# Up-projection of a two-layer decoder: chunk 5 by seven products, and the input's sums begun on GpSimd before the first taps

## The chip, the cores and the metric

The kernel runs on one core of one Trainium2 chip. The metric is the time of one execution on the device in microseconds (us). The core has a matrix engine (TensorE, PE in the profile, with its weight loads shown apart as PEld), a vector engine (VectorE, DVE), a scalar engine (ScalarE, ACT), GpSimd (POOL) and a queue that only starts transfers (SyncE, SP). POOL can compute and can also start transfers. Each engine takes its instructions strictly from its own list; an instruction that has to wait holds up everything behind it on that list.

## The reference, cut to what matters

The model is a trunk of two layers over 512 tokens of width 1024, all in float32. Each layer has an attention part and a gated feed-forward part. The change is in the feed-forward part, which both layers have in the same shape:

```python
def conv_ffn(xn, w_up, cw, cb, w_down):
    a = xn @ w_up                       # (512, 1024) @ (1024, 5632)
    ap = jnp.pad(a, ((0, 0), (CONV_W - 1, 0), (0, 0)))
    a = sum(ap[:, j:j + T] * cw[j] for j in range(CONV_W)) + cb
    gate, val = jnp.split(a, 2, axis=-1)
    return (jax.nn.gelu(gate, approximate=True) * val) @ w_down
```

The 5632 columns of `w_up` are 2816 gate columns and 2816 value columns.

## The kernel before, in words

**Products in three parts.** A float32 product is made of three fast products: each operand is split into a rounded high part and the low remainder, and high x high, high x low and low x high are added up in PSUM (`mm3`, lines 263 to 266). A split costs a rounding copy on ACT (line 57) and a low part. The low part is either a subtraction on DVE (line 69) or, where the lists `ADDED` say so, a copy of the negated weights on ACT (line 64) to which a transfer from the POOL queue adds the raw weights (line 84, "accumulating transfer").

**Chunks.** The up-projection of a layer runs in 22 chunks, c = 0 to 21. A chunk is one block of 128 gate columns and one of 128 value columns. An ordinary chunk needs for each of its two blocks 8 steps of the depth times 3 products of 128x512: 48 matmuls. For chunks 0 and 1 `first_products` (line 533) works in halves of the tokens, since the input's last blocks are still being normalised and transposed.

**Chunks by seven products.** The chunks in `SEVEN` treat depth halves and token halves as a two-by-two scheme of Strassen's kind: seven half-size products instead of eight. Each is 4 steps times 3 matmuls of 128x256 (`half_mm`, line 909): 84 matmuls a chunk. They need sums of the weights and sums of the input.

- The weights' sums: `weights_a(c)` (line 679) makes the first two pairs (A11 and A12, S3 and S2), `weights_b(c)` (line 711) the other ones (S1 and S4, A22). Both are cut into steps by `yield`; in the loop of chunk c the steps of `weights_b(c + 1)` and `weights_a(c + 2)` are taken one at a time between other work (line 936). Two chunks of `SEVEN` that stand side by side are a pair. In the first of a pair, and in one that stands alone, three low parts come by accumulating transfers (`add_low`, lines 671 to 674); in the second of a pair DVE subtracts them (`sub_low`, line 677). Before, the list has four pairs (8 and 9, 11 and 12, 14 and 15, 17 and 18) and chunk 6 alone.
- The input's sums: `sums_in` (line 645), also cut by `yield`. Step one: two additions of 128x2048 on POOL (line 649), high plus low part of the input. Steps two and three: four additions and subtractions on DVE (lines 651, 652, 654, 655). Then four times a rounding copy on ACT and a subtraction on DVE (lines 660 and 661), which give `XA` and `XB`, each with a high part `xsh` and a low part `xsl`. The loop takes one step per block of an ordinary chunk, from chunk 2 on (line 1022). Step one thus stands in chunk 2, behind the first block's products in the text, the last one in chunk 5.

**What follows a chunk.** `taps` (line 610) makes the convolution from the two PSUM banks of the chunk before: per block one pass on ACT (line 614) and two on DVE (lines 615 and 617). `glu` applies the GELU on ACT (line 635), `product` multiplies gate and value on DVE (line 632), and the result goes to memory through the POOL queue (line 630).

**In a chunk by seven products** the order on PE is A11, S3, S2, A22, A12, S1, S4 (lines 952 to 990). DVE and ACT join partial results between these (lines 953, 955, 959, 979, 993, 999). A22 is added onto the bank that holds S3's result, so it may start only when line 955 has read that bank.

**What sets the order.** The text of the kernel is the order of each engine's list; there is no planner. Buffers come from pools with fixed numbers of slots (16 of 8 KB for split weights and inputs, 10 of 4 KB for raw weights, taps and weight sums); an instruction waits when its slot's last user isn't done. The raw weights come through the SP queue (line 49), each load waiting for a slot.

Of the kernel before, what the change touches and what calls it, by code (L numbers as in the profile page):

```python
# [24 lines left out]
BIG = 3.0e38  # L25


SEVEN = 6, 8, 9, 11, 12, 14, 15, 17, 18

ADDED = (4, 5, 7, 10, 13, 16, 20), (4, 5, 20, 21)  # L30
ND = NF // 2
LAST = 3

# [70 lines left out]
def trunk_kernel(ctx, tc, x, norm_gains, w_qkv_a, w_o_a, w_q_b, w_o_b, kv_norm, w_kvf, b_f,  # L104
# [11 lines left out]
    def t8(shape, dt=F32, name="t8"):  # L116
        return p8.tile(shape, dt, tag="t8", name=name)
# [487 lines left out]
    def ffn(l, bd, cp, nxt, ahead):  # L605
# [19 lines left out]
        def product():  # L625

            if gated:
                c, bb = gated.pop()
                if c - 1 in hc:
                    pool.dma_start(hD[c - 1], hc.pop(c - 1))  # L630
                hc[c] = t2([128, T], name="hc")
                dve.tensor_tensor(hc[c], bb[:, 0, :], bb[:, 1, :], ALU.mult)

        def glu(c, bb):
            act.activation(bb[:, 0, :], bb[:, 0, :], AF.Gelu_apprx_tanh)
            gated.append((c, bb))

        def post(c, banks, between=None):
            product()
            glu(c, taps(c, banks, between))  # L640
# [4 lines left out]
        def sums_in():  # L645

            v = [t8([128, 4, T], name=f"xsum{i}") for i in range(2)]
            for i in range(2):
                pool.tensor_tensor(v[i], xT[0][i].bitcast(F32), xT[1][i].bitcast(F32), ALU.add)
            yield  # L650
            dve.tensor_tensor(v[0][:, :, LO], v[0][:, :, HI], v[0][:, :, LO], ALU.subtract)
            dve.tensor_tensor(v[0][:, :, HI], v[1][:, :, HI], v[0][:, :, HI], ALU.subtract)
            yield
            dve.tensor_tensor(v[1][:, :, HI], v[1][:, :, HI], v[0][:, :, LO], ALU.subtract)
            dve.tensor_tensor(v[1][:, :, LO], v[1][:, :, LO], v[1][:, :, HI], ALU.subtract)
            yield
            for X, src in ((XA, v[0]), (XB, v[1])):
                X += [t8([128, 4, T], F32R, name="xsh"), t8([128, 4, T], F32R, name="xsl")]
                for k in (0, 2):
                    act.copy(X[0][:, k:k + 2], src[:, k:k + 2])  # L660
                    dve.tensor_tensor(X[1][:, k:k + 2], src[:, k:k + 2], X[0][:, k:k + 2].bitcast(F32), ALU.subtract)
                    yield
# [8 lines left out]
        def add_low(w, raw):  # L671

            act.activation(w[:, 1], raw, AF.Copy, scale=-1.0)
            pool.dma_start(w[:, 1], raw, accum_op=ALU.add)
# [4 lines left out]
        def weights_a(c):  # L679


            if c >= NF:
                return
            if c not in SEVEN:
                for i in range(2):
                    if c in ADDED[i]:
                        W.high_added()
# [9 lines left out]
            act.copy(w[0][:, 0], r0)  # L697
            if c - 1 not in SEVEN:
                add_low(w[0], r0)
# [3 lines left out]
            dve.tensor_tensor(sa[:, 512:1024], sb[:, 0:512], a11, ALU.subtract)  # L703
            if c - 1 not in SEVEN:
                act.copy(w[1][:, 0], sa)
# [5 lines left out]
        def weights_b(c):  # L711

            if c not in SEVEN:
                return
            (w0, w1), r0, a12, a22, sa, sb = rest.pop(c)
            if c - 1 in SEVEN:
                act.copy(w1[:, 0], sa)
# [3 lines left out]
            act.copy(w[1][:, 0, 0:512], a22)  # L721
            if c - 1 in SEVEN:
                sub_low(w1, sa)
# [195 lines left out]
        base = W.n_get  # L919
        first = first_products(bd, 4)  # L920
        xT = bd.xT
        post(0, first[0:2])
        post(1, first[2:4])
        W.ahead = 1
        W.split(base + 8)
        extra = sums_in()
        steps = iter(())
        begun = None
        before = None
        for c in range(2, NF):  # L930
            if c == NF - 4:
                pair_load(0)
            if c == NF - 3:
                sums = down_sums([(l, ND - 1), (1, 8 + l)], in_one, pool, 1, 0)
                next(sums)
            steps = chain(steps, weights_b(c + 1), weights_a(c + 2))
            if c in SEVEN:
                w = halves.pop(c)
                W.n_get += 2
                x11, x21, x22 = [(xT[0][i], xT[1][i], s) for i, s in ((0, LO), (1, LO), (1, HI))]  # L940
                if begun:
                    banks, s1, s17 = begun
                else:
                    banks = [bank([128, T], name="up") for _ in range(2)]
                    s1, s17 = (t2([128, 256], name="csum") for _ in range(2))
                s12 = t2([128, 256], name="csum")
                o1, o2, o3, o4 = banks[0][:, LO], banks[0][:, HI], banks[1][:, LO], banks[1][:, HI]

                def prod(o, a, x, start=False, w=w):
                    half_mm(o, w[a], x[0:2], x[2], start)  # L950

                def begin():
                    act.copy(s1, o1)
                    prod(o3, "S3", (*XA, HI), True)
                    dve.tensor_tensor(s17, o3, s1, ALU.add)
                    prod(o2, "S2", (*XB, HI))

                def join():
                    dve.tensor_tensor(s12, o2, s1, ALU.add)

                if begun:
                    prod(o2, "S2", (*XB, HI))
                    product()
                    join()
                    bb = taps(*before)
                else:
                    prod(o1, "A11", x11, True)
                    product()
                    bb = taps(*before, begin)
                    join()  # L970
                prod(o3, "A22", (*XB, LO))
                prod(o1, "A12", x21)
                prod(o2, "S1", (*XA, LO))
                next(steps, None)
                glu(before[0], bb)
                next(steps, None)
                if c + 1 in SEVEN:
                    next(steps, None)
                dve.tensor_tensor(o4, o2, s17, ALU.add)
                if c + 1 in SEVEN:  # L980
                    begun = ([bank([128, T], name="up") for _ in range(2)],
                             *(t2([128, 256], name="csum") for _ in range(2)))
                    b1, b3 = (o[:, LO] for o in begun[0])
                    prod(b1, "A11", x11, True, halves[c + 1])
                    act.copy(begun[1], b1)
                    prod(b3, "S3", (*XA, HI), True, halves[c + 1])
                else:
                    begun = W.get(), bank([128, T], name="up")
                    up(*begun, range(4))
                prod(o2, "S4", x22)  # L990
                if c + 1 not in SEVEN:
                    next(steps, None)
                dve.tensor_tensor(o3, o3, s12, ALU.add)
                if c + 1 in SEVEN:
                    late.pop()()
                    dve.tensor_tensor(begun[2], b3, begun[1], ALU.add)
                else:
                    next(steps, None)
                dve.tensor_tensor(o2, o2, s1, ALU.add)  # L999
            else:  # L1000
                banks = [bank([128, T], name="up") for _ in range(1 if begun else 2)]
                if begun:
                    w, first = begun
                    banks = [first, *banks]
                for s in range(2):
                    if s == 0 and begun:
                        up(*begun, range(4, KD))
                        begun = None
                    else:
                        up(W.get(), banks[s], range(KD))  # L1010
                    if c == NF - 2:
                        next(sums)
                    if s == 0 and before:
                        product()
                        bb = taps(*before, (lambda: pair_lows(0)) if c == NF - 1 else None)
                        next(steps, None)
                        glu(before[0], bb)
                        if c >= NF - 2:
                            pair_highs(c - NF + 2)
                            pair_sums(c - NF + 3)  # L1020
                    next(steps, None)
                    next(extra, None)

            if c + 1 not in SEVEN or c + 2 in SEVEN:
                run(steps)
            before = c, banks
            if c == NF - 3:
                pair_sums(0)
# [641 lines left out]
    for n in range(N + 3):  # L1670
        live = n < N
        if live:
# [3 lines left out]
            s = f_scores(j, i)  # L1676
# [83 lines left out]
```

## Time and profile before

| | us |
|---|---|
| median of three runs | 1116.84 |
| lowest and highest | 1116.65 and 1117.51 |
| the profiled execution | 1116.29 |
| its span, first to last instruction | 1114.5 |

The mean granted clock of TensorE in the profiled execution is 0.999. Besides the span, PE's busy time and the stretches of the up-projection matter here. Layer 0's feed-forward part begins with `first` at 179.80 us and its ordinary chunks 2 to 5 run from 204.55 us to 248.10 us; the one of layer 1 has chunk 2 start at 791.87 us.

A row of the timeline gives the start, the duration of all its merged instructions, the engine, the line, what is written and read, the shape and the count, and in brackets how long the engine was idle before it and who ended that. Matmuls overlap one another in the pipeline: a single one shows 0.39 us or 0.28 us, while the next starts 0.23 us or 0.12 us later. What a chunk costs is therefore read from start to start.

### The profile page before, as it was taken

What the parts mean: (1) busy time and instruction counts of PE and PEld (TensorE: products, weight loads), DVE (VectorE), ACT (ScalarE), POOL (GpSimd) and SP (SyncE); (2) the same over time, 40 slices, a digit from 0 to 9 for tenths busy, and PEclk for the clock granted to TensorE, in tenths of its full rate; (3) what the DMA queues carried; (4) which work ended last, traced back from release to release, by engine and by line L of the source; (5) the groups of instructions that cost most, each with busy time, mean ns of one, the idle gap of its engine ahead of it and who ended that gap; (6) DMA issues with size and microseconds to landing.
All of it is one profiled execution on the core that took longest, in us unless ns stands there. A gap on an engine that the chain in (4) does not pass through costs nothing.

```text
span 1114.5 us, 17752 instructions
## 1 busy us (share of the span) xinstructions
PE 1104.6 (99%) x6402; PEld 954.3 (86%) x6402; DVE 866.0 (78%) x1456; ACT 663.5 (60%) x1092; POOL 219.4 (20%) x321
## 2 busy tenths in 40 slices
PE   9999999999999999999999999999999999999997
PEld 6988889889999988888878888789989999988886
DVE  6567788577778799897697776848577778799894
ACT  5454575476666647576562688746465665647572
POOL 2832100421111121000001545500411111121000
PEclk9999999999999999999999999999999999999999
DMA  9469854388878899793447666374388878899862
GB/s 325 152 224 405 314 178 139 85 204 191 203 189 201 238 338 379 268 328 107 133 151 278 195 169 165 112 201 124 86 198 200 189 201 190 243 331 376 297 246 76
DMA packets 185521, 240.43 MB, mean 216 GB/s; under 512 B 11929, under 2 KB 131721, under 8 KB 185434
## 3 DMA queue, kind: packets, MB, share of 16 engines
q1 hardware_dynamic: 169594, 183.99, 50.5%
q0 software_dynamic: 15840, 55.32, 21.2%
q8 instruction: 50, 0.82, 0.3%
q14 instruction: 37, 0.30, 0.1%
HBM read 166.08 MB, written 39.63 MB: 185 GB/s over the span
## 4 chain that ended last, share of the span: by engine, by line
PE 94%; issue 2%; DVE 2%; POOL 1%; ACT 1%; DMA 0%; DVEq 0%; POOLq 0%
PE up L265 13%; PE up L264 13%; PE up L266 13%; PE acc L264 8%; PE acc L266 8%; PE acc L265 8%; PE qk_ps L265 2%; PE qk_ps L264 2%; PE qk_ps L266 2%; PE v_ps L264 2%; PE v_ps L266 2%; PE v_ps L265 2%; PE o_ps L1642 2%; PE s_ps L1594 1%; PE first L266 1%
## 5 line engine op out<-in xcount | busy, mean ns | idle before, releaser
L264 PE MATMUL acc<-w 128*128 128x512 f32 (+1 forms) x311 | 120.6, 388 | 0.3 <-DVE mix L326 0.3
L266 PE MATMUL acc<-w 128*128 128x512 f32 (+1 forms) x311 | 120.4, 387 | 0.0
L57 ACT CAST w<-wraw 128x1024 fp32r<-128x1024 f32 x102 | 104.8, 1048 | 15.7 <-PE v_ps L265 6.9
L69 DVE TENSOR_TENSOR w<-wraw,w 128x1024 fp32r<-128x1024 f32 x76 | 91.8, 1231 | 15.5 <-ACT w L57 15.0
L265 PE MATMUL acc<-w 128*128 128x512 f32 (+1 forms) x267 | 103.2, 387 | 0.0
L265 PE MATMUL up<-xbl,w 128*128 128x512 f32 (+1 forms) x284 | 99.2, 349 | 0.0
L265 PE MATMUL up<-xcl,w 128*128 128x512 f32 (+1 forms) x284 | 99.2, 349 | 0.0
L264 PE MATMUL up<-xbh,w 128*128 128x512 f32 (+1 forms) x284 | 99.1, 349 | 0.0
L264 PE MATMUL up<-xch,w 128*128 128x512 f32 (+1 forms) x284 | 99.1, 349 | 0.0
L266 PE MATMUL up<-xbh,w 128*128 128x512 f32 (+1 forms) x284 | 99.0, 349 | 0.0
L266 PE MATMUL up<-xch,w 128*128 128x512 f32 (+1 forms) x284 | 99.0, 349 | 0.0
L614 ACT ACTIVATE bb<-up,conv 128x512 f32<-128x512 f32 x80 | 59.8, 775 | 64.8 <-DVE up L999 33.6
L264 PE MATMUL up<-xsh,w 128*128 128x256 f32 x288 | 81.5, 283 | 0.0
L265 PE MATMUL up<-xsl,w 128*128 128x256 f32 x288 | 81.5, 283 | 0.0
L266 PE MATMUL up<-xsh,w 128*128 128x256 f32 x288 | 81.5, 283 | 0.0
L84 POOL DMA_DIRECT2D w<-wraw x26 | 24.7, 956 | 284.8 <-ACT w L64 248.4
L264 PEld LDWEIGHTS acc<-w 128*128 128x128 f32 x311 | 58.4, 188 | 12.5 <-DVE mix L326 0.7
L266 PEld LDWEIGHTS acc<-w 128*128 128x128 f32 x311 | 58.4, 188 | 11.9
L615 DVE SCALAR_TENSOR_TENSOR bb<-up,conv,bb 128x511 f32<-128x511 f32 x80 | 59.5, 744 | 7.1 <-ACT bb L614 7.1
L617 DVE SCALAR_TENSOR_TENSOR bb<-up,conv,bb 128x510 f32<-128x510 f32 x80 | 59.9, 749 | 2.8
L264 PEld LDWEIGHTS up<-xbh,w 128*128 128x128 f32 x284 | 53.8, 189 | 7.0
L264 PEld LDWEIGHTS up<-xch,w 128*128 128x128 f32 x284 | 53.8, 189 | 7.0
(315 smaller groups left out, 3165.5 us busy)
## 6 DMA issues: line engine op xcount, KB each, us to landing
wraw<-in_w_up_dram SPq DMA_DIRECT2D x88, 512.0 KB
w<-wraw POOLq DMA_DIRECT2D x36, 512.0 KB, 7.3
dT<-dsums SPq DMA_DIRECT2D x24, 512.0 KB
dsums<-in_w_down_dram SPq DMA_DIRECT2D x22, 512.0 KB
dsums<-in_w_down_dram SPq DMA_DIRECT2D x44, 256.0 KB
hD<-hc POOLq DMA_DIRECT2D x44, 256.0 KB, 7.2
dact<-hD SPq DMA_DIRECT2D x44, 256.0 KB
wraw<-dT SPq DMA_DIRECT2D x22, 512.0 KB
```

Of the source, the lines that this page charges most:

```text
L57: self.nc.scalar.copy(pair[:, 0], raw)
L69: self.nc.vector.tensor_tensor(pair[:, 1], raw, pair[:, 0].bitcast(F32), ALU.subtract)
L84: self.nc.gpsimd.dma_start(pair[:, 1], raw, accum_op=ALU.add)
L264: pe.matmul(o, ah, bh, start=first, stop=False, skip_group_check=shared)
L265: pe.matmul(o, ah, bl, start=False, stop=False, skip_group_check=shared)
L266: pe.matmul(o, al, bh, start=False, stop=last, skip_group_check=shared)
L614: act.activation(bb[:, s, :], ps, AF.Identity, bias=cp[:, 3, ch:ch + 1], scale=cp[:, 2, ch:ch + 1])
L615: dve.scalar_tensor_tensor(bb[:, s, 1:], ps[:, :T - 1], cp[:, 1, ch:ch + 1], bb[:, s, 1:], ALU.mult, ALU.add)
L617: dve.scalar_tensor_tensor(bb[:, s, 2:], ps[:, :T - 2], cp[:, 0, ch:ch + 1], bb[:, s, 2:], ALU.mult, ALU.add)
L1594: pe.matmul(s[hh][:, :nn], qT[j][:, m, hh, i * 128:(i + 1) * 128], k, start=m == 0, stop=m == 1)
L1642: pe.matmul(o[64 * hh:64 * hh + 64, i * 128:(i + 1) * 128], Vt[hd // 8][:, k, (hd % 8) * 64:(hd % 8) * 64 + 64], pT[j, i, hh][:, k, :], st ...
```

## The change

Chunk 5 joins `SEVEN`, so it is the first of a pair with chunk 6, which no longer stands alone; its two entries in `ADDED` go. There are then ten chunks by seven products per layer.

`sums_in` is started before the taps of chunk 0: its first step, the two additions on POOL, is now issued directly behind the first products and thus ahead of everything that POOL does for chunks 2 and later. The loop takes two steps instead of one behind each ordinary chunk's first block, so that steps two and three stand in chunk 2 behind its first block, the first `XA` step behind its second block, two more steps behind chunk 3's first block and the last one behind chunk 3's second block.

```diff
-SEVEN = 6, 8, 9, 11, 12, 14, 15, 17, 18
-
-ADDED = (4, 5, 7, 10, 13, 16, 20), (4, 5, 20, 21)
+SEVEN = 5, 6, 8, 9, 11, 12, 14, 15, 17, 18
+
+ADDED = (4, 7, 10, 13, 16, 20), (4, 20, 21)
@@ in ffn @@
         first = first_products(bd, 4)
         xT = bd.xT
+        extra = sums_in()
+        next(extra)
         post(0, first[0:2])
         post(1, first[2:4])
         W.ahead = 1
         W.split(base + 8)
-        extra = sums_in()
         steps = iter(())
@@ in the loop over chunks, behind an ordinary chunk's block s @@
                     next(steps, None)
                     next(extra, None)
+                    if s == 0:
+                        next(extra, None)
```

## The prediction, made before the changed kernel ran

> **What bounds the kernel now.** I read the page first (busy shares, slices, chain), then PE's own waits, then the stretches of the up-projection, then single rows.
>
> ```profile
> span 1114.5 us, 17752 instructions
> ...
> PE 1104.6 (99%) x6402; PEld 954.3 (86%) x6402; DVE 866.0 (78%) x1456; ACT 663.5 (60%) x1092; POOL 219.4 (20%) x321
> ...
> PEclk9999999999999999999999999999999999999999
> ...
> PE 94%; issue 2%; DVE 2%; POOL 1%; ACT 1%; DMA 0%; DVEq 0%; POOLq 0%
> ```
>
> ```profile
> PE warm L231 <- DVE zero L226: 1.4, 1, 1.4
> PE pT_ps L1627 <- ACT w L57: 0.6, 1, 0.6
> PE pT_ps L1627 <- DVE nm L1603: 0.4, 1, 0.4
> ```
>
> TensorE is busy 99% of the span at the full clock and carries 94% of the chain that ended last. Its longest waits are in the second fence, and none of these three is in an up-projection. So there is nothing to gain there by removing waits: time goes only if PE gets less to do, and it comes back at once if the change makes PE wait. The stretches say what a chunk costs:
>
> ```profile
> core 0: us, PE busy (x) PEld busy (x) DVE busy (x) ACT busy (x) POOL busy (x), PEclk, DMA share, GB/s
> 204.55:248.10 43.55, 43.55 (x194) 36.05 (x193) 29.99 (x32) 27.37 (x33) 17.13 (x12) 1.00 0.67 154
> 248.10:258.20 10.10, 10.10 (x80) 9.84 (x79) 7.79 (x13) 5.86 (x9) 2.28 (x3) 1.00 1.01 238
> 269.10:300.18 31.08, 31.08 (x217) 29.16 (x216) 25.03 (x40) 19.51 (x26) 5.12 (x9) 1.00 0.83 195
> ```
>
> ```profile
> 237.22 0.39 PE L264 MATMUL up<-xbh,w 128*128 128x512 f32 x1
> 248.10 0.28 PE L264 MATMUL up<-xbh,w 128*128 128x256 f32 x1
> 269.10 0.28 PE L264 MATMUL up<-xbh,w 128*128 128x256 f32 x1
> 300.18 0.28 PE L264 MATMUL up<-xbh,w 128*128 128x256 f32 x1
> 824.31 0.39 PE L266 MATMUL up<-xch,w 128*128 128x512 f32 x1
> 856.19 0.39 PE L266 MATMUL up<-xch,w 128*128 128x512 f32 x1
> 887.27 0.39 PE L266 MATMUL up<-xch,w 128*128 128x512 f32 x1
> ```
>
> The first stretch is the ordinary chunks 2 to 5: PE is busy all of its 43.55 us, 43.55 / 4 = 10.89 us a chunk, 10.89 / 48 = 0.227 us a matmul. The third is a pair and the ordinary chunk behind it (8, 9, 10), also without a gap: 31.08 us. The rows are the first matmuls of chunks 5, 6, 8 and 11, and in layer 1 the last matmuls ahead of chunks 5, 8 and 11.
>
> **The change part by part: PE.** Chunks 5, 6, 7 were ordinary, seven, ordinary, and become seven, seven, ordinary, which is what 8, 9, 10 are now. In layer 0 the three take 269.10 - 237.22 = 31.88 us before and should take 31.08 us: 0.80 us less. In layer 1 856.19 - 824.31 = 31.88 us against 887.27 - 856.19 = 31.08 us: 0.80 us again. By matmuls: 48 x 0.227 = 10.89 us go, and 84 x (31.08 - 10.89) / 168 = 10.10 us come. **Sum on PE: -1.6 us.** Everything else has to stay hidden under PE; whether it does is the rest of the work.
>
> **The additions on POOL** move past the POOL queue's transfers for chunk 4 and past the taps of chunks 0 and 1.
>
> ```profile
> L649 POOL TENSOR_TENSOR xsum<-xbh,xbl x2: 4934/4936/4937, 210.0 to 214.6; 128x2048 f32<-128x2048 f32 x2
> L651 DVE TENSOR_TENSOR xsum<-xsum x2: 5628/5628/5629, 215.0 to 802.1; 128x1024 f32<-128x1024 f32 x2
> L652 DVE TENSOR_TENSOR xsum<-xsum,xsum x2: 1225/1225/1225, 220.7 to 807.8; 128x1024 f32<-128x1024 f32 x2
> L660 ACT CAST xsh<-xsum x8: 1030/1035/1050, 226.5 to 832.9; 128x1024 fp32r<-128x1024 f32 x8
> L661 DVE TENSOR_TENSOR xsl<-xsum,xsh x8: 1218/1222/1226, 227.7 to 834.0; 128x1024 fp32r<-128x1024 f32 x8
> ```
>
> ```profile
> 28.23 1.11 POOL L1059 CAST xph<-xah 128x512 fp32r<-128x512 f32 x1
> 29.27 2.15 POOL L1059 CAST xpl<-xal 128x512 fp32r<-128x512 f32 x1
> 27.18 1.29 DVE L356 TENSOR_TENSOR xal<-xt_ps,xah 128x512 fp32r<-128x512 f32 x2 [1.28 <-ACT xah L355]
> 28.62 1.79 DVE L69 TENSOR_TENSOR w<-wearly,w 128x1024 fp32r<-128x1024 f32 x1 [0.16 <-ACT w L57]
> ```
>
> The two additions take 4.94 us each. Line 651 does the work of line 652 and takes 4.4 us longer, because it began beside the second addition. The other fence shows how such a meeting goes: DVE's subtraction (28.62 to 30.41) with both inputs in SBUF ran only once POOL's copy had ended at 29.34, and POOL's next copy, 2.15 us instead of 1.11 us, ran only once DVE was done. They take turns by whole instructions. The two subtractions of line 356, with one input in PSUM, lie beside POOL's copies at 0.64 us each: not held up.
>
> ```profile
> 190.55 1.29 DVE L356 TENSOR_TENSOR xbl<-xt_ps,xbh 128x512 fp32r<-128x512 f32 x2 [0.88 <-ACT xbh L355]
> 191.98 1.23 DVE L69 TENSOR_TENSOR w<-wraw,w 128x1024 fp32r<-128x1024 f32 x1
> 196.99 0.75 DVE L615 SCALAR_TENSOR_TENSOR bb<-first,conv,bb 128x511 f32<-128x511 f32 x1 [3.78 <-ACT bb L614]
> 201.75 0.69 DVE L632 TENSOR_TENSOR hc<-bb 128x512 f32<-128x512 f32 x1 [0.41 <-ACT bb L635]
> 207.02 1.22 DVE L69 TENSOR_TENSOR w<-wraw,w 128x1024 fp32r<-128x1024 f32 x1
> 219.11 1.23 POOL L84 DMA_DIRECT2D w<-wraw  x1
> ```
>
> The input's halves are complete at 191.2 us and 191.8 us (line 356). The first addition then runs from about 191.3 us to 196.2 us; line 69 behind line 356 waits for it and ends near 197.4 us instead of 193.2 us, where DVE was idle for 3.78 us; the taps start 0.4 us late. The second addition ends near 202.3 us, and line 632 waits about 0.5 us for it. Cost on the path: nothing, for the next chunks' weights that line 69 splits are used by PE at 215.4 us (204.55 + 10.89), and DVE is idle from 208.2 us. Were DVE kept out until both additions end, it would be 5 us late at 197 us and caught up near 212 us; still nothing. Nothing in the trace says when the two slots for the sums come free. If only with the end of the first products, at 204.55 us, the additions end near 214.4 us and the steps below are some 6 us later, which their cover of 12 us still holds. The accumulating transfer that stood behind the additions at 219.11 us goes out near 211 us.
>
> **The sums' DVE and ACT steps** run from 208.2 us, POOL no longer in their way. DVE has until chunk 5 starts at 237.2 us: four sums of 1.22 us, four of line 661 (4.9 us), two sets of taps (8 x 0.75 us), three products (0.69 us), and weight sums:
>
> ```profile
> L700 DVE TENSOR_TENSOR wsum<-wraw x5: 682/683/687, 232.3 to 297.6; 128x512 f32<-128x512 f32 x5
> L725 ACT CAST w<-wsum x4: 1052/1055/1058, 243.8 to 297.1; 128x1024 fp32r<-128x1024 f32 x4
> DMA to landing us min/median/max: 4.6/5.6/8.1
> ```
>
> Eight operations as line 700 (four sums and a half split for chunk 5, three sums for chunk 6): 5.4 us. Together 4.9 + 4.9 + 6.0 + 2.1 + 5.4 = 23.3 us in 29 us. In order: the four sums end near 213, the first XA subtraction at 214, the taps of chunk 2 near 218 (their second bank ends at 226.3 - 10.89 = 215.4), the first weight sums at 220, the last XB subtraction near 226. S3 and S2 need XA and XB at 238.7 us and 240.1 us: 12 us to spare. Cost: nothing.
>
> **The weights of chunk 5.** Gone per layer are two rounding copies, two negations and two transfers for chunk 5; three and a half copies, three negations, three transfers, five sums and the five small joins come. Chunk 6, now second of a pair, loses three negations and three transfers and gets three subtractions of 1.22 us on DVE. ACT's load hardly moves, POOL starts two transfers fewer, DVE gains about 8 us in work and loses the 4.4 us of line 651. The raw loads on SP are the same, at most one step later, and a chunk ahead of use. The latest piece is S1's low part. DVE's sum for it follows the taps of chunk 3, near 230 us; copy and negation (line 725, 1.05 us each) end near 232.3 us, and the transfer lands after 5.6 us, at most 8.1 us: 238 to 240.4 us. PE comes to S1 after five products, 237.2 + 5 x 10.10 / 7 = 244.4 us: 4 to 6.5 us to spare. Price if that cover goes: one for one, each microsecond beyond 244.4, in both layers. If it were merely as late as chunk 6's transfer stands now relative to its chunk, PE would still not wait, as it does not in the stretch at 248.10. I take nothing; the upper bound is in the third rival.
>
> **Sum.** 1114.5 - 1.6 = 1112.9 us of span, 1116.29 - 1.6 = 1114.7 us for an execution like the profiled one, which lies 0.55 us under the median. Against the median: 1116.84 - 1.6 = **1115.2 us**, 0.14% less. Its own range is 1114.6 to 1115.8, from the spread of the runs before (1116.65 to 1117.51).
>
> **Rivals.** *Faster by over 0.2%*: half as wide a matmul costs half, 0.227 / 2 = 0.1135 us, so that chunk 5 takes 84 x 0.1135 = 9.53 us and 2 x (10.89 - 9.53) = 2.7 us go: 1114.1 us. Against it stands the measured 31.08 us of a pair and its neighbour, which gives 0.120 us. The Trainium skill ("TensorE: Matmul & The Clock Gate", section Back-to-back issue gap) lists 262 cycles for 256 columns and 518 for 512, nearly that half; by it 2 x (10.89 - 84 x 0.227 x 262 / 518) = 2.5 us would go, and the trace disagrees with 0.120 against 0.115 us. Chance 0.04.
>
> *The gain is eaten*: the handshake in chunk 5 costs PE some 0.8 us a layer. A22 may not start before DVE's join has read S3's bank, 1.4 us after S3 ends, and that join is behind a tap on DVE and a copy on ACT. For it: DVE has more to do here than in any chunk before. Against it: the same order in chunks 6 and 8 leaves PE without a gap in the stretches above, and DVE comes to chunk 5 early. 1115.2 + 2 x 0.8 = 1116.8 us. Chance 0.10.
>
> *Slower*: S1's low part lands late. The stretch at 248.10 has its DMA engines busy 1.01 of the time, so a landing could double, 16.2 us: 232.3 + 16.2 = 248.5 us, 4.1 us of waiting per layer, 1115.2 + 8.2 = 1123.4 us. It decides from (1.6 + 2.2) / 2 = 1.9 us of waiting a layer, a landing after 246.3 us. Against it: 8.1 us is the longest landing shown, and the stretch before chunk 5 has a DMA share of 0.67. Chance 0.08.
>
> **How the numbers follow.** The forecast has 0.78. A measurement of this kernel can tell about 0.2%, 2.2 us, from no change: faster is under 1114.6 us, slower over 1119.1 us. Faster: 0.04 and an edge of 0.06 of the forecast, 0.10. Slower: 0.08 and 0.02 for an eaten gain that goes further, 0.10. Same: 0.80. The range takes in the forecast, the eaten gain and half of the way to the first rival: 1114.3 to 1117.3 us.
>
> **What would show it.** Right: PE without a gap from 204.55 us to chunk 8, chunk 8's start 0.8 us earlier, 31.08 us from chunk 5 to 8; line 649 from about 191 us; line 651 at 1.2 us; line 69 near 192 us at about 5.4 us; the last line 661 near 226 us. Wrong: a PE wait at S3 (sums late), at A22 (joins late) or at S1 (transfer late), in both layers alike, or additions that start only when the first products end.

## The result, and the profile after

| | before | changed |
|---|---|---|
| median, us | 1116.89 (16 runs, 1116.29 to 1118.69) | 1114.88 (16 runs, 1114.45 to 1115.77) |
| the profiled execution, us | 1116.29 | 1115.42 |
| its span, us | 1114.5 | 1113.6 |

The ratio is 0.998 with a 95% interval of 0.9973 to 0.9988: 2.0 us less, about the 0.2% that a measurement of this kernel can tell from no change, with an interval that leaves 1 out. A second measurement of the same kernel (e8 below) gave 1114.72 us and 0.9981 (0.9972 to 0.999).

The page of the changed kernel:

```profile
span 1113.6 us, 17913 instructions
...
PE 1103.1 (99%) x6474; PEld 956.6 (86%) x6474; DVE 883.3 (79%) x1482; ACT 664.4 (60%) x1094; POOL 217.3 (20%) x317
```

PE has 1.5 us less to do (1104.6 - 1103.1), in 72 matmuls more, and is still busy 99% of the span. DVE has 17.3 us more to do and its time is hidden. POOL's busy time falls by 2.1 us.

The stretches of the changed kernel (columns: PE, PEld, DVE, ACT, POOL busy, granted clock, DMA share, GB/s). The first is chunks 2 to 4, the second chunks 5 to 7:

```profile
core 0: us, PE busy (x) PEld busy (x) DVE busy (x) ACT busy (x) POOL busy (x), PEclk, DMA share, GB/s
204.53:237.19 32.66, 32.66 (x146) 27.03 (x145) 26.11 (x32) 21.99 (x26) 6.20 (x8) 1.00 0.63 137
237.19:268.27 31.08, 31.08 (x217) 29.16 (x216) 23.55 (x37) 18.97 (x25) 4.49 (x7) 1.00 0.72 179
```

Single rows of its timeline: the first matmuls of chunks 5 and 8, in layer 0 and then in layer 1.

```profile
237.19 0.28 PE L264 MATMUL up<-xbh,w 128*128 128x256 f32 x1
...
268.27 0.28 PE L264 MATMUL up<-xbh,w 128*128 128x256 f32 x1
...
823.71 0.28 PE L264 MATMUL up<-xch,w 128*128 128x256 f32 x1
...
854.78 0.28 PE L264 MATMUL up<-xch,w 128*128 128x256 f32 x1
```

Chunks 5, 6 and 7 take 31.08 us in layer 0 and 31.07 us in layer 1, where they took 31.88 us. PE has no gap in either stretch, at a clock of 1.00.

What PE waits for in the changed kernel (total, times, longest):

```profile
PE s_ps L1597 <- DMA qst<-qst: 1.1, 2, 0.8
PE up L266 <- DMA w<-wraw: 0.5, 1, 0.5
```

The second row is new in the up-projection: in this one execution chunk 10 of layer 1 waited 0.5 us for the low part of its gate weights, which an ordinary chunk gets by an accumulating transfer. In e8 the same kernel has no such wait and a span of 1112.9 us. Between two profiles that have no wait in the up-projection the span thus shrinks by 1114.5 - 1112.9 = 1.6 us.

The moved additions, the DVE rows around them and S1's transfer:

```profile
191.29 10.20 POOL L649 TENSOR_TENSOR xsum<-xbh,xbl 128x2048 f32<-128x2048 f32 x2 [52.33 <-DVE xbl L356]
...
191.95 5.05 DVE L69 TENSOR_TENSOR w<-wraw,w 128x1024 fp32r<-128x1024 f32 x1
...
201.72 0.69 DVE L632 TENSOR_TENSOR hc<-bb 128x512 f32<-128x512 f32 x1 [0.41 <-ACT bb L635]
...
208.14 1.22 DVE L651 TENSOR_TENSOR xsum<-xsum 128x1024 f32<-128x1024 f32 x1
...
222.92 3.50 DVE L661 TENSOR_TENSOR xsl<-xsum,xsh 128x1024 fp32r<-128x1024 f32 x3 [3.01 <-ACT xsh L660]
...
233.08 0.85 POOL L674 DMA_DIRECT2D w<-wsum  x1 [9.41 <-DVE wsum L703]
```

The additions start as soon as the input is complete, and nothing holds back their slots. Line 69 takes 5.05 us instead of 1.23 us: it gets its turn between the two additions. Line 651 takes 1.22 us instead of 5.63 us. The last line 661 ends at 226.4 us. The transfers of the weight sums in the stretch from 215 to 245 us, from issue to landing:

```profile
DMA to landing us min/median/max: 5.2/5.4/5.5
```

S1's low part thus lands at 238.6 us (issue 233.08 us, 5.5 us), and PE's first product with it starts at 244.62 us: 6.0 us to spare.

PE's last matmul of the whole kernel, in the kernel before, in e1 (below: the move of the sums without chunk 5) and in e8 (the changed kernel again):

```profile
1107.77 0.28 PE L266 MATMUL acc<-w 128*128 128x256 f32 x1
```

```profile
1107.79 0.28 PE L266 MATMUL acc<-w 128*128 128x256 f32 x1
```

```profile
1106.19 0.28 PE L266 MATMUL acc<-w 128*128 128x256 f32 x1
```

PE is done 1.58 us earlier in e8 than before, which is the 1.6 us of the up-projection; in e1 it is done when it was before. What follows PE's last matmul up to the end of the span takes 6.4 us before, in the changed kernel and in e8, but 5.8 us in e1 and in e12, the same kernel again.

### The profile page after: what moved, and what is told of

Same layout as the page of the kernel before. It is cut to its first block, busy times and chain, and to the rows that moved or that the text cites. A ratio compares the mean times of both kernels' runs of the same rounds, so it can differ in the third digit from the quotient of the medians.

```text
span 1113.6 us, 17913 instructions
## 1 busy us (share of the span) xinstructions
PE 1103.1 (99%) x6474; PEld 956.6 (86%) x6474; DVE 883.3 (79%) x1482; ACT 664.4 (60%) x1094; POOL 217.3 (20%) x317
## 4 chain that ended last, share of the span: by engine, by line
PE 87%; DVE 4%; issue 3%; DMA 3%; ACT 2%; POOL 1%; DVEq 0%; POOLq 0%; ACTq 0%
PE up L266 12%; PE up L264 12%; PE up L265 12%; PE acc L264 8%; PE acc L265 8%; PE acc L266 8%; PE qk_ps L265 2%; PE qk_ps L264 2%; PE qk_ps L266 2%; PE v_ps L264 2%; PE v_ps L266 2%; PE v_ps L265 2%; PE first L266 1%; PE first L264 1%; PE first L265 1%
## 5 line engine op out<-in xcount | busy, mean ns | idle before, releaser
L69 DVE TENSOR_TENSOR w<-wraw,w 128x1024 fp32r<-128x1024 f32 x76 | 99.3, 1327 | 14.5 <-ACT w L57 14.0
L57 ACT CAST w<-wraw 128x1024 fp32r<-128x1024 f32 x98 | 100.6, 1047 | 15.7 <-PE v_ps L265 6.9
L266 PE MATMUL up<-xch,w 128*128 128x512 f32 (+1 forms) x280 | 96.3, 344 | 0.5 <-DMA w<-wraw 0.5
L265 PE MATMUL up<-xcl,w 128*128 128x512 f32 (+1 forms) x280 | 96.3, 344 | 0.0
L265 PE MATMUL up<-xbl,w 128*128 128x512 f32 (+1 forms) x280 | 96.3, 344 | 0.0
L264 PE MATMUL up<-xch,w 128*128 128x512 f32 (+1 forms) x280 | 96.3, 344 | 0.0
L264 PE MATMUL up<-xbh,w 128*128 128x512 f32 (+1 forms) x280 | 96.3, 344 | 0.0
L266 PE MATMUL up<-xbh,w 128*128 128x512 f32 (+1 forms) x280 | 96.2, 344 | 0.0
L264 PE MATMUL up<-xsh,w 128*128 128x256 f32 x320 | 90.6, 283 | 0.0
L265 PE MATMUL up<-xsl,w 128*128 128x256 f32 x320 | 90.6, 283 | 0.0
L266 PE MATMUL up<-xsh,w 128*128 128x256 f32 x320 | 90.6, 283 | 0.0
L264 PEld LDWEIGHTS up<-xsh,w 128*128 128x128 f32 x320 | 61.4, 192 | 0.0
L265 PEld LDWEIGHTS up<-xsl,w 128*128 128x128 f32 x320 | 61.4, 192 | 0.0
L266 PEld LDWEIGHTS up<-xsh,w 128*128 128x128 f32 x320 | 61.4, 192 | 0.0
```

Source lines behind the costliest of these rows:

```text
L57: self.nc.scalar.copy(pair[:, 0], raw)
L69: self.nc.vector.tensor_tensor(pair[:, 1], raw, pair[:, 0].bitcast(F32), ALU.subtract)
L264: pe.matmul(o, ah, bh, start=first, stop=False, skip_group_check=shared)
L265: pe.matmul(o, ah, bl, start=False, stop=False, skip_group_check=shared)
L266: pe.matmul(o, al, bh, start=False, stop=last, skip_group_check=shared)
```

## The experiments

All edits are against the changed kernel. All these kernels compute the whole result; where fills are put in, they write a scratch tile that nothing reads. Medians of the kernel before beside them lay at 1116.83 to 1117.09 us.

**e8: the changed kernel again**, without an edit.

> The changed kernel once more, beside the kernel before on the same chip and beside the run with ordinary lows on DVE. Theory, 1.6 us of TensorE's work: ratio 0.9986. If the move of the sums brings something of its own as well: ratio 0.998 or less, as first measured.

1114.72 us (11 runs, 1114.44 to 1115.45), ratio 0.9981 (0.9972 to 0.999). The gain repeats. It and the first measurement, 1114.72 to 1114.88 us, are what the others are compared with below; where one number is needed it is 1114.8 us.

**e3: the size of a chunk's gain.** Chunks 5 and 6 are both ordinary, so that eight chunks per layer go by seven products; the sums stay early.

```diff
-SEVEN = 5, 6, 8, 9, 11, 12, 14, 15, 17, 18
-ADDED = (4, 7, 10, 13, 16, 20), (4, 20, 21)
+SEVEN = 8, 9, 11, 12, 14, 15, 17, 18
+ADDED = (4, 5, 6, 7, 10, 13, 16, 20), (4, 5, 6, 20, 21)
```

> The changed kernel with chunks 5 and 6 both ordinary (eight chunks by seven products), their low parts by accumulating transfers. Theory, 0.80 us per chunk and layer: 2 x 1.6 = 3.2 us slower than the changed kernel, 1.6 us slower than before, 1118.1 us against 1114.9. Rival, that a chunk is worth half of 0.227 us a matmul, 1.36 us per chunk and layer: 5.4 us slower than the changed kernel, 1120.3 us.

1118.27 us (11 runs, 1117.3 to 1119.54), ratio 1.0008 (0.9999 to 1.0017): 3.4 to 3.55 us above the changed kernel. Two chunks in two layers make four, so 0.85 to 0.89 us a chunk. That is the 0.80 us of the rows within the spread of the runs; if half as wide a matmul cost half, it would be 1.36 us a chunk and 5.4 us together. That rival falls. Single rows say the same: layer 0's up-projection, from the start of its first matmul to the end of its last, takes 211.55 us here, 210.79 us with nine chunks (e1 below) and 209.99 us with ten (e8), without a wait of PE in any of the three: 0.76 and 0.80 us a chunk.

**e1 and e12: the move alone.** Chunk 5 is ordinary again, with its two transfers; the sums stay early. This kernel was measured twice.

```diff
-SEVEN = 5, 6, 8, 9, 11, 12, 14, 15, 17, 18
-ADDED = (4, 7, 10, 13, 16, 20), (4, 20, 21)
+SEVEN = 6, 8, 9, 11, 12, 14, 15, 17, 18
+ADDED = (4, 5, 7, 10, 13, 16, 20), (4, 5, 20, 21)
```

> Only the second half of the change: the input's sums begin directly behind the first products and take two steps per block, but chunk 5 stays ordinary (nine chunks by seven products). Theory, that the gain is TensorE's work alone and the earlier sums cost and bring nothing: within 0.4 us of the kernel before, about 1116.9 us. Rival, that part of the measured 2.0 us comes from the sums' move itself (DVE no longer held up for 4.4 us at line 651, POOL's transfers no longer behind the additions): 0.4 to 1 us faster than before, 1116.5 us or less.

> The run with only the sums moved, once more. Theory (the move alone brings nothing): 1116.9 us, ratio 1.000 with an interval that holds it. Rival (the move alone brings something, as the first ratio of 0.9993 leaves open): a ratio of 0.9993 or less again.

1116.02 us (11 runs, 1115.57 to 1118.04), ratio 0.9993 (0.9984 to 1.0002); and 1116.01 us (11 runs, 1115.62 to 1117.67), ratio 0.9991 (0.9982 to 1.0). Each interval by itself still reaches 1, but both put the move at about -1.0 us, where the prediction had nothing. With e3, eight, nine and ten chunks with early sums make a ladder: 1118.27, 1116.0, 1114.8 us, 1.7 us per chunk and both layers against 1.6 us predicted. By medians, the 2.0 us then split into about 1.0 us for the move and 1.2 us for chunk 5 (1116.0 - 1114.8), each uncertain by some tenths.

The profiles show where much of the move's part lies, and it isn't in the up-projection. PE takes 210.79 and 210.79 us for the two up-projections before, 210.79 and 210.85 us in e1, and its last matmul of the kernel starts at 1107.77 and at 1107.79 us. The span of e1 is 0.6 us shorter (1113.9 against 1114.5 us) because what follows PE's last matmul takes 5.8 us instead of 6.4 us. Both profiles of this kernel have 5.8 us there, both of the changed kernel 6.4 us. Why a build has one or the other isn't shown; the edit touches nothing there. So of the 1.0 us some 0.6 us lie behind the last matmul, and they are gone again in the changed kernel, which is why the step from 1116.0 to 1114.8 us is less than chunk 5's 1.6 us.

What remains is about 0.4 us of the medians, in the move alone as in the whole change (2.0 - 1.6), and it isn't explained. A candidate is the transfer for chunk 7's gate low part: it landed 0.3 us ahead of its use before (256.9 against 257.2 us) and some 3 us ahead in e1 (253.9 against 257.1 us), so in other executions than the profiled one, which is the fastest of its 16, it might come late before. That is argued only, and no run tests it: e7, next, takes such transfers out of the changed kernel, not out of the kernel before.

**e7: without the ordinary chunks' transfers.** The gate low parts of chunks 7, 10, 13 and 16 are subtracted on DVE.

```diff
-ADDED = (4, 7, 10, 13, 16, 20), (4, 20, 21)
+ADDED = (4, 20), (4, 20, 21)
```

> The changed kernel, but the gate block's low part of the ordinary chunks 7, 10, 13 and 16 is subtracted on DVE (1.22 us) instead of being made by a negation on ACT and an accumulating transfer. In the profile of the changed kernel this transfer landed 0.6 us late in chunk 10 of layer 1, the only wait in its up-projections. Theory, that this wait is all there is to win: 0.3 to 0.8 us faster than the changed kernel, 1114.2 to 1114.6 us. Rival, that DVE, which is busy 25 us of 31 us there, falls behind and TensorE waits for a join: 1116 us or more.

1114.89 us (11 runs, 1113.92 to 1115.33), ratio 0.9979 (0.997 to 0.9988), against 1114.72 us of e8 on the same chip: no difference. Waits such as chunk 10's 0.5 us aren't worth anything that a median shows.

**e2: the additions at their old place.** Chunk 5 goes by seven products, but the sums start in chunk 2 as before, two steps behind each first block.

```diff
         first = first_products(bd, 4)
         xT = bd.xT
-        extra = sums_in()
-        next(extra)
...
         W.split(base + 8)
+        extra = sums_in()
         steps = iter(())
```

> Only the first half of the change: chunk 5 by seven products, with the sums begun where they were, in chunk 2 behind its first block, two steps per block from there so that they are complete in time at all. Theory: the additions on POOL end near 219.5 us instead of 202 us, line 651 is held up to 220.6 us again, DVE is some 7 us later in chunk 4, the transfer for S1 starts near 239.5 us instead of 233.1 us and lands at 245 to 247.5 us against 244.4 us, and XB's last step meets S2; TensorE waits 0.5 to 3 us in each layer, so 1 to 6 us slower than the changed kernel: 1116 to 1121 us. Rival, that the move was not needed, since the cover of 12 us for the sums and 4 to 6.5 us for S1 holds: 1114.9 us, no wait on TensorE.

1131.83 us (4 runs, 1130.22 to 1133.72), ratio 1.0128 (1.0113 to 1.0144): 17 us above the changed kernel. PE's waits in e2, and its timeline (line 953 of e2 is line 954 of the changed kernel):

```profile
PE up L264 <- ACT csum L953: 10.0, 2, 5.1
PE up L264 <- DVE csum L955: 1.5, 2, 0.8
```

```profile
233.21 3.49 DVE L661 TENSOR_TENSOR xsl<-xsum,xsh 128x1024 fp32r<-128x1024 f32 x3 [3.01 <-ACT xsh L660]
...
240.11 0.68 DVE L720 TENSOR_TENSOR wsum<-wraw,wsum 128x512 f32<-128x512 f32 x1
...
243.79 1.23 DVE L661 TENSOR_TENSOR xsl<-xsum,xsh 128x1024 fp32r<-128x1024 f32 x1 [2.40 <-ACT xsh L660]
...
240.82 1.04 ACT L725 CAST w<-wsum 128x1024 fp32r<-128x1024 f32 x1 [1.35 <-DVE wsum L720]
...
242.73 1.03 ACT L660 CAST xsh<-xsum 128x1024 fp32r<-128x1024 f32 x1
...
245.29 0.36 ACT L953 COPY csum<-up 128x256 f32<-128x256 f32 x1
...
240.33 0.28 PE L266 MATMUL up<-xsh,w 128*128 128x256 f32 x1
245.70 0.58 PE L264 MATMUL up<-xsh,w 128*128 128x256 f32 x1 [5.08 <-ACT csum L953]
...
246.29 0.41 PE L266 MATMUL up<-xsh,w 128*128 128x256 f32 x1
246.51 0.41 PE L264 MATMUL up<-xsh,w 128*128 128x256 f32 x1
```

The same places in the changed kernel:

```profile
229.82 0.68 DVE L720 TENSOR_TENSOR wsum<-wraw,wsum 128x512 f32<-128x512 f32 x1
...
230.54 1.06 ACT L725 CAST w<-wsum 128x1024 fp32r<-128x1024 f32 x1 [1.07 <-DVE wsum L720]
...
238.82 0.37 ACT L954 COPY csum<-up 128x256 f32<-128x256 f32 x1 [4.66 <-PE up L266]
```

In e2 the additions run from 210.4 to 219.9 us and line 651 takes 5.63 us again. DVE is 10.3 us late from there on, at line 661 (233.21 against 222.92 us) as at line 720. ACT's cast of line 725 waits for line 720 and is as late. Behind it on ACT stands the copy of A11's result (line 953). S2 goes into the bank that holds A11's result, so PE may not start S2 before that copy. In the changed kernel the copy had 4.66 us of idle ACT ahead of it. In e2 that idle time is used up, and one more copy of line 660 stands in the line: 10.3 - 4.66 + 0.95 = 6.6 us later, as the rows show (245.29 - 238.82 = 6.5 us). PE stands for 5.25 us (245.70 - 240.33 - 0.12). The rest of the 6.5 us is 0.8 us that the copy had to spare in the changed kernel, where S2 starts at 240.06 us, and 0.4 us by which all of e2 is later.

The copy isn't the only bound that this order breaks. The sums' last step stands one block later in the text here, in chunk 4 instead of chunk 3, and the last line 661 ends at 245.0 us (243.79 + 1.23) instead of 226.4 us. S2's third and fourth depth steps multiply what it makes. S2's eighth matmul, the first to need it, would have been due near 241.3 us, so without the wait for the copy PE would still have stood for some 3.7 us (an estimate from these rows). The expectation had named this bound, and the late S1, but not the copy; and its 1116 to 1121 us were too low by far.

The stretches of e2, same columns as above:

```profile
240.00:246.00 6.00, 0.92 (x7) 0.71 (x6) 3.60 (x6) 5.17 (x7) 1.42 (x2) 0.76 0.37 76
246.00:249.00 3.00, 2.63 (x12) 2.33 (x11) 2.93 (x6) 1.89 (x3) 0.00 (x0) 0.50 0.59 154
249.00:253.30 4.30, 3.92 (x18) 3.92 (x19) 4.26 (x7) 1.07 (x2) 0.00 (x0) 0.50 0.41 121
253.30:260.00 6.70, 6.70 (x58) 6.70 (x57) 3.68 (x6) 2.89 (x4) 1.42 (x2) 1.00 0.88 242
```

Behind the wait the granted clock is 0.50 until about 253.3 us, and matmuls follow each other in 0.213 us instead of 0.120 us. The profiled execution, the slowest of e2's four, has a span 19.0 us above e8's (1131.9 against 1112.9 us). The two layers' waits are 11.5 us of it, and 30 slow matmuls in layer 0 and 38 in layer 1, at 0.093 us each, some 6.3 us. So the early start is no side matter: with the sums begun and spread as in e2, chunk 5 by seven products makes the kernel 15 us slower than before.

**e4: an eleventh chunk.** Chunks 5, 6 and 7 in a row and then pairs.

```diff
-SEVEN = 5, 6, 8, 9, 11, 12, 14, 15, 17, 18
-ADDED = (4, 7, 10, 13, 16, 20), (4, 20, 21)
+SEVEN = 5, 6, 7, 9, 10, 12, 13, 15, 16, 18, 19
+ADDED = (4, 8, 11, 14, 17, 20), (4, 20, 21)
```

> The changed kernel with eleven chunks by seven products: 5, 6 and 7 side by side, then pairs 9 and 10, 12 and 13, 15 and 16, 18 and 19. Theory, if the third of a run stays covered as the second does: 1.6 us faster than the changed kernel, 1113.3 us. Rival: DVE, which is busy 25.03 us of the 31.08 us of a pair with its neighbour, gets a third chunk in a row whose low parts it subtracts, falls behind, and TensorE waits at A22 or S1 in the run, or the down-projection's start behind chunk 19 gets in the way: 1115 us or more.

1130.23 us (4 runs, 1129.22 to 1132.34), ratio 1.0116 (1.01 to 1.0131). PE's waits in e4:

```profile
PE up L266 <- DMA w<-wraw: 5.3, 4, 1.4
PE acc L266 <- DVE w L767: 3.5, 2, 1.8
PE acc L265 <- DVE w L767: 2.8, 2, 1.4
```

The first row is the low part of ordinary chunks behind a group, chunk 8 first (1.39 us). The other two are the start of the down-projection, where DVE's low parts of the weights come late:

```profile
422.31 0.50 PE L265 MATMUL acc<-w 128*128 128x512 f32 x1 [1.38 <-DVE w L767]
424.58 0.79 PE L266 MATMUL acc<-w 128*128 128x512 f32 x1 [1.76 <-DVE w L767]
```

Behind these two short waits, with a single matmul between them, the granted clock is 0.50 from 424 to 430 us, and matmuls of 512 columns take 0.427 us instead of 0.227 us. The waits of 11.6 us and the slow matmuls behind them, and not PE's own work, are the price. One chunk more isn't to be had by the list alone.

**e5 and e6: S1's transfer late.** 8 and 18 fills of 128x512 on POOL ahead of the transfer of S1's low part in chunk 5, to learn how much cover it has.

```diff
-                add_low(w[0], sb)
+                act.activation(w[0][:, 1], sb, AF.Copy, scale=-1.0)
+                if c == 5:
+                    idle = t2([128, 512], name="idle")
+                    for _ in range(8):
+                        pool.memset(idle, 0.0)
+                pool.dma_start(w[0][:, 1], sb, accum_op=ALU.add)
```

> The changed kernel, with eight fills of a scratch tile put on POOL ahead of the accumulating transfer for S1 of chunk 5, in both layers: that transfer alone starts some 4 us later (estimated from a fill of a quarter of the size, 0.2 us), at 237 instead of 233.1 us, and lands at about 242.5 us against 244.4 us. Theory (the transfer has 4 to 6 us to spare): no wait on TensorE, the time of the changed kernel, 1114 to 1116 us. Rival (the spare time is less than computed): a wait of TensorE at S1 in each layer, 1117 us or more.

> The same with eighteen fills: the transfer for S1 starts some 9 us later and lands at about 248 us, 3.5 us after TensorE comes to S1. As the prediction priced it, one for one: 7 us over the two layers, 1122 us. Rival, from the run with the sums at their old place (the granted clock fell to 0.50 behind a wait of 5 us): the wait is followed by matmuls at half clock and costs clearly more than its own length, 1125 us or more. Had the transfer no part in it: 1115 us.

One run each, 1114.82 and 1114.94 us, and neither tells anything. POOL in e6:

```profile
223.26 10.81 POOL L733 MEMSET idle<- 128x512 f32 x18
234.04 0.85 POOL L734 DMA_DIRECT2D w<-wsum  x1
```

The fills ran in the time in which POOL waited for ACT's negation anyway, so the transfer started 0.1 us (e5, 233.19 us) and 1.0 us (e6) later than the changed kernel's 233.08 us.

**e9, e10, e11: S1's transfer late, tied to its own source.** Now the first fill waits for a small copy on ACT behind the negation, with 8, 14 and 20 fills.

```diff
+                    act.activation(idle[:, 0:8], sb[:, 0:8], AF.Copy, scale=-1.0)
+                    for _ in range(8):
```

> In the two runs before, the fills on POOL ran ahead of time, while POOL waited for the negation, and delayed nothing. Here they write a tile that ACT touches behind the negation, so they start with it. Eight fills of 0.58 us (start to start in the run with eighteen) put the transfer for S1 at 237.9 us and its landing at 243.4 us; TensorE needs the low part with S1's third matmul, 244.6 us. Theory: no wait, 1114.8 us. Rival (less to spare than computed): a wait.

> The same with fourteen fills: the transfer starts at 241.4 us and lands at 246.9 us, 2.3 us after TensorE needs it, in each layer. One for one, as predicted: 1114.8 + 4.6 = 1119.4 us. Rival, that any such wait also halves the granted clock for some us: 1122 us or more.

> The same with twenty fills: the transfer starts at 244.9 us and lands at 250.4 us, 5.8 us late, in each layer. One for one: 1114.8 + 11.6 = 1126.4 us. Rival, from the run with the sums at their old place, where a wait of 5 us was followed by matmuls at half clock, some 3.5 us more: 1114.8 + 2 x 9.3 = 1133 us, with a granted clock of 0.5 behind the wait.

One run each: 1114.54, 1118.03 and 1129.95 us. The timelines of e9, e10 and e11 in this order:

```profile
237.10 0.84 POOL L735 DMA_DIRECT2D w<-wsum  x1
```

```profile
241.02 0.84 POOL L735 DMA_DIRECT2D w<-wsum  x1
...
244.76 0.28 PE L265 MATMUL up<-xsl,w 128*128 128x256 f32 x1
245.63 0.39 PE L266 MATMUL up<-xsh,w 128*128 128x256 f32 x1 [0.58 <-DMA w<-wsum]
245.85 0.28 PE L264 MATMUL up<-xsh,w 128*128 128x256 f32 x1
```

```profile
244.17 0.84 POOL L735 DMA_DIRECT2D w<-wsum  x1
...
244.41 0.28 PE L265 MATMUL up<-xsl,w 128*128 128x256 f32 x1
249.44 0.58 PE L266 MATMUL up<-xsh,w 128*128 128x256 f32 x1 [4.75 <-DMA w<-wsum]
249.82 0.42 PE L264 MATMUL up<-xsh,w 128*128 128x256 f32 x1
```

A transfer 4.0 us late (e9) costs nothing. At 7.9 us (e10) PE loses 0.75 us in layer 0 (245.63 - 244.76 - 0.12) and 1.6 us in layer 1, and goes on at 0.120 us a matmul. That is 2.4 us of the 3.2 us measured over 1114.8 us, in a single run. At 11.1 us (e11) PE loses 4.9 us and 6.6 us, and what follows is at half speed. PE's waits in e11, and the stretches with layer 0's wait and behind it:

```profile
PE up L266 <- DMA w<-wsum: 11.2, 2, 6.5
```

```profile
244.70:250.50 5.80, 1.05 (x5) 1.06 (x6) 1.21 (x2) 2.46 (x3) 2.30 (x4) 0.68 0.87 162
250.50:257.00 6.50, 6.50 (x45) 6.50 (x45) 2.41 (x4) 0.37 (x1) 0.00 (x0) 0.76 1.04 273
```

The measured 15.2 us (1129.95 - 1114.8) are these 11.2 us of waits, 0.6 us of another, and some 3.4 us from matmuls that take 0.213 us behind both waits, in layer 0 until about 253.3 us, with a granted clock of 0.50 from 249.4 us on. The sum lies between the 1126.4 us of one for one and the rival's 1133 us. So S1's cover is between 4.0 and 7.9 us, as the 6.0 us of the rows said. A single wait is paid about one for one up to 1.6 us, and from some length on (at 4.9 us for certain) with the half clock on top. The Trainium skill ("TensorE: Matmul & The Clock Gate", section "HAM oscillation — how this bites in real kernels") puts the bound at idle gaps of some 3.4 us; 1.6 us without and 4.9 us with a drop agree with it. The length of one wait isn't the whole of it, though: in e4 the clock fell behind waits of 1.38 and 1.76 us with one matmul between them.

## Why the prediction was right

The forecast was 1115.2 us in 1114.3 to 1117.3 us and "same" within 0.2%; measured were 1114.88 us and, again, 1114.72 us. Its mechanism stood; one of its prices and one claimed cover did not.

- **PE's term, right.** 31.88 to 31.08 us per layer: 31.08 and 31.07 us. PE's last matmul of the kernel starts 1.58 us earlier in e8 than before. The ladder of e3, e1 and the changed kernel gives 1.7 us per chunk and both layers by medians, against the term of 1.6 us.
- **The additions, right.** Start at 191.29 us (191.3 predicted), line 69 pushed to 197.0 us (197.4), taking turns with DVE by whole instructions. The Trainium skill ("SBUF — State Buffer", section "SBUF: two separate sides") calls the port pair that both use an exclusive lock for a whole instruction; the 5.05 us of a 1.23 us subtraction agree. One step was too dark: the second addition ended at 201.5 us, not 202.3 us, so line 632 at 201.72 us did not wait its 0.5 us. Costing the additions at nothing was right.
- **Line 651, right**: 1.22 us instead of 5.63 us, and the last line 661 at 226.4 us (226 predicted).
- **S1's transfer, right**: issue 233.1 us (232.3), landing 238.6 us (238 to 240.4), 6.0 us to spare (4 to 6.5). e9 to e11 confirm the cover.
- **"One for one", too low.** It holds up to 1.6 us of waiting; 4.9 us brought a half clock behind it, about 1.7 us more a layer in e11. The third rival, with 4.1 us a layer, might for that reason have been priced too low; no run had just that wait.
- **"Which their cover of 12 us still holds", not borne out.** The step costed a start at 204.55 us, with everything 6 us later, at nothing, since only XA and XB were compared with PE. In e2 the lateness is 10.3 us, within the 12 us, and yet PE stood for 5.25 us: the nearest bound was ACT's copy of A11's result behind a cast that waits for DVE. (The last low part of the sums was 18.6 us late there, beyond the 12 us, but only because its step stands later in e2's text.) The copy's cover was 5.5 us, of which 4.66 us are ACT's idle time and 0.8 us lie between the copy and S2's start. An estimate from these rows for the 6 us of that step is 6 - 5.5 = 0.5 us of waiting a layer. The case didn't come up, since the slots were free at once.
- **The rival "the gain is eaten" by the handshake** did not happen in the changed kernel: PE has no gap in chunk 5. But e2 shows that the handshake breaks first when DVE is late, and at an earlier point than the rival named: 5.1 us at S2, and only then 0.8 us at A22.
- **The move, costed at nothing**, measured about -1.0 us twice, with intervals that just touch no change. On PE it is nothing, as costed: the up-projections take the same time and the last matmul comes at the same time. About 0.6 us of it lie behind the last matmul, which the prediction didn't look at, and the changed kernel doesn't have them. The measured 2.0 us has an interval that includes the sum's 1.6 us (a ratio of 0.9986), so the sum isn't refuted. What the remaining 0.4 us is, and whether it is anything, stays open.

## What to carry to other kernels

On a kernel whose matrix engine is busy 99% of the time, a chunk's gain can be read from an identical stretch that is there already, start to start, and it arrives in full as long as nothing else on the chain is late. For the cover, follow a late engine through every queue that waits for it, up to the first instruction that PE needs; the operand with the obvious deadline need not be the one that fails. Price a PE wait of several microseconds, or two shorter ones close together, at more than its length. And before a difference under 1 us is credited to an edit, compare where PE's last matmul ends: here two builds differed by 0.6 us behind it.

## What the runs showed of the hardware that was not expected

- **Half clock behind short waits.** After single waits of 4.9 us (e11) and 5.25 us (e2) in an otherwise gapless stream the granted clock was 0.50, in layer 0 until about 253.3 us, which is 4 us after the restart in e11 and 7.6 us in e2 (with a second wait of 0.8 us in between). Matmuls of 256 columns took 0.213 us instead of 0.120 us. After single waits of 0.75 and 1.6 us (e10) it stayed at 1.00. Waits of 1.38 and 1.76 us with one matmul between them (e4) brought it to 0.50 for some 6 us.
- **Lateness travels undiminished.** In e2 DVE's 10.3 us at line 661 still stood at 10.3 us at line 720, since DVE's list had no idle time between them that the lateness could use; it shrank only at ACT's 4.66 us of idle time.
- **Fills do not delay what waits anyway.** 10.8 us of fills moved a transfer by 1.0 us, as POOL had been idle for 9.4 us ahead of it. A delay has to be tied to the same event as the work that it is to hold back.
